# Two of a summed pair's four weight additions made by an accumulating DMA from DRAM, and eight raw weight slabs in flight instead of seven

## The chip, the core and the metric

The kernel runs on one core of a Trainium2 chip. The metric is device time in microseconds for one execution, the median of several runs. Engines are named as in the profile: PE (TensorE matmuls), PEld (its weight loads), DVE (VectorE), ACT (ScalarE), POOL (GpSimd) and SP (which only issues transfers here).

## The reference, cut to what matters

A trunk of two layers over 256 positions of width 2048, in float32. Each layer is a mixer followed by a feed-forward block; the change touches the feed-forward blocks alone.

```python
D_MODEL, SEQ, DEPTH = 2048, 256, 2
D_FF = 4 * D_MODEL

def rmsnorm(x, g):
    y = x * lax.rsqrt(jnp.mean(x * x, axis=-1, keepdims=True) + EPS)
    return y * g

for l in range(DEPTH):
    g = norm_g[l]
    u = rmsnorm(h, g[0])
    ...
    h = h + rmsnorm(y, g[1])
    u = rmsnorm(h, g[2])
    z = jnp.square(jax.nn.relu(u @ mlp_w1[l])) @ mlp_w2[l]
    h = h + rmsnorm(z, g[3])
```

## The kernel before

**Precision.** The weights come as float32. Every weight slab is split into a rounded part `whi`, which ScalarE makes by a cast, and the residual `wlo`, which VectorE makes by subtracting `whi` from the raw slab. A product then takes three matmuls: left high with `whi`, left high with `wlo`, left low with `whi`.

**Tiling.** A raw slab holds 128 partitions by two rows of 512 columns, 512 KB. Raw slabs live in a pool of `RAW_BUFS` buffers (line 25), which SP fills ahead of use. `whi` and `wlo` have `W_BUFS` = 6 buffers each (line 26). A buffer is free again when TensorE has made its last product with it, so ScalarE and VectorE can run at most six such tiles ahead of TensorE.

**The feed-forward block.** The hidden width of 8192 is cut into eight chunks of 1024 columns. The loop in `mlp` runs the up projection of chunk c, then the down projection of chunk c-1. Chunk 0 uses plain blocks; chunks 1 to 7 of each layer, 14 in all, use the class `Pairs` for the up projection. The down projection (class `Block`, lines 220 to 238) takes 16 slabs, each with one cast (L223), one residual (L224) and 12 matmuls (L236 to L238).

**Pairs.** The up projection of a chunk walks over eight pairs of k tiles in the order of the string `PAIRS = "CSCSSCSS"`. One pair is a 2 by 2 block of weight tiles (two k tiles, two halves of 512 columns, L and R) times a 2 by 2 block of activations (two k tiles, two halves of the positions). A C pair makes it conventionally, with 8 products (24 matmuls). An S pair, called a summed pair here, makes it in Strassen's manner with 7 products (21 matmuls), which need sums of weight tiles. For these, `Pairs.load` does the following. The raw slabs L and R are loaded (L327). L is split as it is (`plain`), and of R the second row (`r1`). Then four additions on VectorE (line 336) build the sums in place: R's second row takes R's first, R's first row takes L's first, L's first row takes the new second row of R, and L's second row takes the new first row of L. The new R is split (`two`) after the second addition, and the new L (`four`) after the last. So a summed pair fills four weight buffers, in the order plain, r1, two, four, and a C pair fills two. The casts are line 331 and the residuals line 332.

`Pairs.mm` makes the products (L357 to L359). A summed pair begins with the two products of `plain`, then one of `r1`, two of `two` and two of `four`. After the last pair of a chunk, VectorE and ScalarE combine the sums into the four blocks of the result (L372, L383, L387, L397, L398, L598).

**What sets the order.** The kernel is written as one program, and a scheduler lays it out on the engines. Each engine then runs its list in order: an instruction that waits holds up everything behind it on that engine. POOL issues nothing in the chunks before the change; its list there is empty between the stores of `mid` and `hsave` (L532).

Of the kernel before, what the change touches and what calls it, by code (L numbers as in the profile page):

```python
# [14 lines left out]
ALU = mybir.AluOpType  # L15
# [6 lines left out]
EPS = 1e-6  # L22
NT = 2
SLAB = 2
RAW_BUFS = 7
W_BUFS = 6
LEAD = 6
PAIRS = "CSCSSCSS"
# [11 lines left out]
def trunk(ctx, tc, x, x_t, norm_g, ng_cols, e_win, rbf, e_wout, o_win, lbraw, smalls, wa2, ba, o_wout, w1, w2,  # L40
          c_ident, c_flip, c_mask, out):
    nc = tc.nc
# [3 lines left out]
    x2p = ctx.enter_context(tc.tile_pool(name="x2p", bufs=8))  # L46
    rawp = ctx.enter_context(tc.tile_pool(name="rawp", bufs=RAW_BUFS))
    wp = ctx.enter_context(tc.tile_pool(name="wp", bufs=W_BUFS))
# [153 lines left out]
    def w_pair():  # L202
        return [wp.tile([P, SLAB, 512], F32R, name="w" + n) for n in ("hi", "lo")]

    class Block:
# [7 lines left out]
        def load(self, s):  # L213
            k0 = self.kts[s * SLAB]
            raw = rawp.tile([P, SLAB, 512], F32, name="raw")
            hi, lo = w_pair()
            n = slice(0, self.n)
            fine = s in self.fine
            for a, b in ((0, 1), (1, 2)) if fine else ((0, SLAB),):
                nc.sync.dma_start(out=raw[:, a:b, n], in_=self.wv[:, k0 + a:k0 + b, self.n0:self.n0 + self.n])  # L220
                if fine:
                    self.beside[a]()
                nc.scalar.copy(out=hi[:, a:b, n], in_=raw[:, a:b, n])  # L223
                nc.vector.tensor_tensor(out=lo[:, a:b, n], in0=raw[:, a:b, n], in1=hi[:, a:b, n], op=ALU.subtract)  # L224
            self.w[s] = (hi, lo)
# [84 lines left out]
    class Pairs:  # L310
# [13 lines left out]
        def load(self, s):  # L324
            raws = [rawp.tile([P, SLAB, 512], F32, name="raw") for _ in range(2)]
            for raw, n in zip(raws, (self.n0, self.n0 + 512)):
                nc.sync.dma_start(out=raw, in_=self.wv[:, 2 * s:2 * s + 2, n:n + 512])  # L327

            def conv(raw, i=slice(0, SLAB)):
                hi, lo = w_pair()  # L330
                nc.scalar.copy(out=hi[:, i, :], in_=raw[:, i, :])  # L331
                nc.vector.tensor_tensor(out=lo[:, i, :], in0=raw[:, i, :], in1=hi[:, i, :], op=ALU.subtract)  # L332
                return hi, lo

            def add(dst, a, b):
                nc.vector.tensor_tensor(out=dst, in0=a, in1=b, op=ALU.add)  # L336

            L, R = raws
            if PAIRS[s] == "C":
                self.w[s] = [conv(L), conv(R)]  # L340
                return
            plain = conv(L)
            r1 = conv(R, slice(1, 2))
            add(R[:, 1, :], R[:, 1, :], R[:, 0, :])
            add(R[:, 0, :], R[:, 0, :], L[:, 0, :])
            two = conv(R)
            add(L[:, 0, :], L[:, 0, :], R[:, 1, :])
            add(L[:, 1, :], L[:, 1, :], L[:, 0, :])
            self.w[s] = [plain, r1, two, conv(L)]
# [863 lines left out]
```

## Time and profile before

| | |
|---|---|
| median of 3 runs | 2261.35 us (2261.01 to 2261.88) |
| the profiled execution's own time | 2261.99 us |
| its span, first to last instruction | 2260.2 us |
| granted TensorE clock | 0.999 |
| ACT busy / DVE busy, share of the span | 52% / 77% |
| read from DRAM, whole span | 430.57 MB |

The span is shorter than the execution's time by 1.8 us, which lie around it. TensorE's matmuls overlap: a row's duration is longer than the distance between the starts of two neighbours, so the pace of TensorE is read from the distance of starts and not from the busy share. In a timeline, a row that ends in "x4" stands for four instructions in a row on that engine, and a bracket shows for how long the engine had been idle and what released it.

### The profile page before, as it was taken

The numbers are of one execution on the slowest core, as the hardware profiler recorded it, in microseconds if no ns is written. First come the engines' busy times: TensorE is split into PE (matmuls) and PEld (weight loads), VectorE is DVE, ScalarE is ACT, GpSimd is POOL, SyncE is SP. The second block draws the span as 40 slices with busy tenths as digits, with TensorE's granted clock in tenths as the row PEclk, the third lists the DMA queues.
The fourth block names the chain that finished last, engine by engine and source line by source line (L and its number), as shares of the span: only waits on it lengthen the run. The fifth ranks groups of instructions, "written<-read, shape, count | busy, mean of one in ns | idle before, by whom it ended". The sixth has DMA issues, their size and how long they took to land.

```text
span 2260.2 us, 28830 instructions
## 1 busy us (share of the span) xinstructions
PE 2238.3 (99%) x10556; PEld 1850.9 (82%) x10556; DVE 1750.7 (77%) x2328; ACT 1173.7 (52%) x1612; POOL 20.7 (1%) x40
## 2 busy tenths in 40 slices
PE   9999999999999999999999999999999999999998
PEld 7888887888888888888788888887888888888886
DVE  6656656988898898896867767657979789789786
ACT  7444445655454454454746454546555445445453
POOL 0000000000000000000100000000000000000000
PEclk9999999999999999999999999999999999999999
DMA  9565576565665665676655555576565565665673
GB/s 344 168 182 168 168 268 186 181 222 165 198 216 160 211 198 184 205 242 221 213 172 166 153 151 153 173 237 194 169 205 195 187 206 184 197 205 177 214 263 102
DMA packets 222559, 440.87 MB, mean 195 GB/s; under 512 B 13744, under 2 KB 14544, under 8 KB 222416
## 3 DMA queue, kind: packets, MB, share of 16 engines
q1 hardware_dynamic: 218880, 429.18, 59.1%
q0 software_dynamic: 2816, 8.99, 1.1%
q8 instruction: 83, 1.36, 0.3%
q10 hardware_dynamic: 720, 0.85, 0.1%
q14 instruction: 60, 0.49, 0.1%
HBM read 430.57 MB, written 8.40 MB: 194 GB/s over the span
## 4 chain that ended last, share of the span: by engine, by line
PE 75%; DVE 14%; issue 5%; ACT 4%; DMA 1%; ACTq 0%; DVEq 0%; SPq 0%
PE acc L237 18%; PE acc L238 17%; PE acc L236 17%; DVE raw L336 4%; DVE wlo L332 4%; PE acc L275 3%; PE aux L275 3%; ACT whi L331 3%; DVE wlo L224 2%; PE aux L272 2%; PE acc L272 2%; DVE ulo L383 2%; PE aux L359 2%; PE aux L357 2%; PE aux L358 2%
## 5 line engine op out<-in xcount | busy, mean ns | idle before, releaser
L224 DVE TENSOR_TENSOR wlo<-raw,whi 128x1024 fp32r<-128x1024 f32 (+1 forms) x561 | 676.2, 1219 | 303.9 <-ACT whi L223 301.9
L223 ACT CAST whi<-raw 128x1024 fp32r<-128x1024 f32 (+1 forms) x561 | 582.5, 1053 | 587.1 <-PE acc L238 464.7
L331 ACT CAST whi<-raw 128x1024 fp32r<-128x1024 f32 x364 | 343.5, 969 | 372.3 <-DVE raw L336 213.8
L237 PE MATMUL acc<-wlo,x 128*128 128x512 f32 x1280 | 502.7, 393 | 1.9 <-DVE wlo L224 0.6
L238 PE MATMUL acc<-whi,x 128*128 128x512 f32 x1280 | 498.8, 390 | 0.0
L236 PE MATMUL acc<-whi,x 128*128 128x512 f32 x1280 | 497.1, 392 | 0.0
L332 DVE TENSOR_TENSOR wlo<-raw,whi 128x1024 fp32r<-128x1024 f32 x364 | 397.9, 1119 | 106.2 <-ACT whi L331 99.4
L237 PEld LDWEIGHTS acc<-wlo,x 128*128 128x128 f32 x1280 | 240.3, 188 | 59.2 <-DVE wlo L224 10.8
L236 PEld LDWEIGHTS acc<-whi,x 128*128 128x128 f32 x1280 | 240.3, 188 | 50.6
L238 PEld LDWEIGHTS acc<-whi,x 128*128 128x128 f32 x1280 | 240.4, 188 | 49.1
L236 PE MATMUL acc<-whi,xt 128*128 128x512 f32 x640 | 254.1, 399 | 0.5 <-ACT xt L671 0.5
L237 PE MATMUL acc<-wlo,xt 128*128 128x512 f32 x640 | 251.6, 394 | 3.0 <-DVE wlo L224 3.0
L238 PE MATMUL acc<-whi,xt 128*128 128x512 f32 x640 | 250.8, 392 | 0.0
L336 DVE TENSOR_TENSOR raw<-raw 128x512 f32<-128x512 f32 x280 | 193.8, 692 | 9.3
L237 PEld LDWEIGHTS acc<-wlo,xt 128*128 128x128 f32 x640 | 120.8, 189 | 29.6 <-DVE wlo L224 6.2
L236 PEld LDWEIGHTS acc<-whi,xt 128*128 128x128 f32 x640 | 120.6, 189 | 25.7 <-ACT xt L671 1.4
L238 PEld LDWEIGHTS acc<-whi,xt 128*128 128x128 f32 x640 | 120.5, 188 | 25.3 <-issue 0.3
L357 PE MATMUL acc<-whi,xt 128*128 128x512 f32 x308 | 120.0, 390 | 0.0
L359 PE MATMUL acc<-whi,xt 128*128 128x512 f32 x308 | 119.8, 389 | 0.0
L358 PE MATMUL acc<-wlo,xt 128*128 128x512 f32 x308 | 119.8, 389 | 0.0
L358 PE MATMUL aux<-wlo,s 128*128 128x512 f32 x280 | 110.6, 395 | 1.9 <-DVE wlo L332 0.2
L357 PE MATMUL aux<-whi,s 128*128 128x512 f32 x280 | 109.2, 390 | 0.0
(230 smaller groups left out, 2551.2 us busy)
## 6 DMA issues: line engine op xcount, KB each, us to landing
raw<-w SPq DMA_DIRECT2D x512, 512.0 KB, 4.5
raw<-o_win SPq DMA_DIRECT2D x112, 512.0 KB, 3.8
raw<-e_win SPq DMA_DIRECT2D x95, 512.0 KB, 3.9
raw<-e_wout SPq DMA_DIRECT2D x32, 512.0 KB, 4.2
raw<-o_wout SPq DMA_DIRECT2D x32, 512.0 KB, 3.7
s<-norm_g SPq DMA_DIRECT2D x8, 512.0 KB, 4.6
mid<-s POOLq DMA_DIRECT2D x8, 512.0 KB, 3.5
s<-mid SPq DMA_DIRECT2D x8, 512.0 KB, 5.7
```

The source lines that it names most:

```text
L223: nc.scalar.copy(out=hi[:, a:b, n], in_=raw[:, a:b, n])
L224: nc.vector.tensor_tensor(out=lo[:, a:b, n], in0=raw[:, a:b, n], in1=hi[:, a:b, n], op=ALU.subtract)
L236: nc.tensor.matmul(ps, xh, hi[:, i, 0:self.n], start=first, stop=False)
L237: nc.tensor.matmul(ps, xh, lo[:, i, 0:self.n], start=False, stop=False)
L238: nc.tensor.matmul(ps, xl, hi[:, i, 0:self.n], start=False, stop=last)
L275: nc.tensor.matmul(self.ps[j], hi[:, i, cs], x, start=s == 0 and i == 0, stop=False)
L331: nc.scalar.copy(out=hi[:, i, :], in_=raw[:, i, :])
L332: nc.vector.tensor_tensor(out=lo[:, i, :], in0=raw[:, i, :], in1=hi[:, i, :], op=ALU.subtract)
L336: nc.vector.tensor_tensor(out=dst, in0=a, in1=b, op=ALU.add)
L357: nc.tensor.matmul(ps, xh, hi[:, i, :], start=first, stop=False)
L358: nc.tensor.matmul(ps, xh, lo[:, i, :], start=False, stop=False)
L359: nc.tensor.matmul(ps, xl, hi[:, i, :], start=False, stop=done and not (n == "bR" and i == 0))
```

## The change

Of the four additions of a summed pair, the first two are replaced by one transfer, issued by POOL, that reads a row of 1024 columns of the weight from DRAM again and adds it to the whole slab R in place. The row holds what L's first row and R's first row held when they were loaded, so the slab receives the same sums. The transfer writes R's second row, which `r1` reads, and so it starts after `r1`'s cast and residual. The other two additions stay on VectorE. Separately, the pool of raw slabs grows from seven buffers to eight.

```diff
-RAW_BUFS = 7
+RAW_BUFS = 8
...
             plain = conv(L)
             r1 = conv(R, slice(1, 2))
-            add(R[:, 1, :], R[:, 1, :], R[:, 0, :])
-            add(R[:, 0, :], R[:, 0, :], L[:, 0, :])
+            nc.gpsimd.dma_start(out=R.rearrange("p a b -> p (a b)"), in_=self.wv[:, 2 * s, self.n0:self.n0 + 1024],
+                                accum_op=ALU.add)
             two = conv(R)
             add(L[:, 0, :], L[:, 0, :], R[:, 1, :])
             add(L[:, 1, :], L[:, 1, :], L[:, 0, :])
             self.w[s] = [plain, r1, two, conv(L)]
```

The new transfer has line 344 in the changed kernel; the two additions that stay, the casts and the residuals keep lines 336, 331 and 332.

VectorE's list before the change, in the fifth of the first layer's paired chunks: the second summed pair and the beginning of the third. Slab raw_6904 is L and raw_6905 is R of the second pair, raw_6949 and raw_6950 are those of the third.

```order
L332 TENSOR_TENSOR wlo_6909<-raw_6904,whi_6908 128x1024
L332 TENSOR_TENSOR wlo_6913<-raw_6905,whi_6912 128x512
L336 TENSOR_TENSOR raw_6905<-raw_6905 128x512
L336 TENSOR_TENSOR raw_6905<-raw_6905,raw_6904 128x512
L336 TENSOR_TENSOR raw_6904<-raw_6904,raw_6905 128x512
L336 TENSOR_TENSOR raw_6904<-raw_6904 128x512
L332 TENSOR_TENSOR wlo_6919<-raw_6905,whi_6918 128x1024
L332 TENSOR_TENSOR wlo_6925<-raw_6904,whi_6924 128x1024
L332 TENSOR_TENSOR wlo_6954<-raw_6949,whi_6953 128x1024
L332 TENSOR_TENSOR wlo_6958<-raw_6950,whi_6957 128x512
```

The same place on VectorE in the changed kernel; here raw_6883 and raw_6884 are L and R of the second pair, raw_6927 and raw_6928 those of the third.

```order
L332 TENSOR_TENSOR wlo_6888<-raw_6883,whi_6887 128x1024
L332 TENSOR_TENSOR wlo_6892<-raw_6884,whi_6891 128x512
L336 TENSOR_TENSOR raw_6883<-raw_6883,raw_6884 128x512
L336 TENSOR_TENSOR raw_6883<-raw_6883 128x512
L332 TENSOR_TENSOR wlo_6897<-raw_6884,whi_6896 128x1024
L332 TENSOR_TENSOR wlo_6903<-raw_6883,whi_6902 128x1024
L332 TENSOR_TENSOR wlo_6932<-raw_6927,whi_6931 128x1024
L332 TENSOR_TENSOR wlo_6936<-raw_6928,whi_6935 128x512
L336 TENSOR_TENSOR raw_6927<-raw_6927,raw_6928 128x512
L336 TENSOR_TENSOR raw_6927<-raw_6927 128x512
```

Two of the four rows of line 336 are gone, and nothing else has taken their place: the first addition that is left reads R's new second row, and it stands directly behind the residual that the transfer waits for.

ScalarE's list in the changed kernel, from the same second summed pair to the end of the third; its order is the one that it had.

```order
L331 CAST whi_6887<-raw_6883 128x1024
L331 CAST whi_6891<-raw_6884 128x512
L331 CAST whi_6896<-raw_6884 128x1024
L331 CAST whi_6902<-raw_6883 128x1024
L331 CAST whi_6931<-raw_6927 128x1024
L331 CAST whi_6935<-raw_6928 128x512
L331 CAST whi_6940<-raw_6928 128x1024
L331 CAST whi_6946<-raw_6927 128x1024
```

The third row casts R after the transfer, and the two casts of the next pair (raw_6927, raw_6928) stand behind it and behind the cast of the summed L.

TensorE's list in the third summed pair before the change, from the first product with the summed R (whi_6963, wlo_6964) to the end; whi_6969 and wlo_6970 are the summed L.

```order
L357 MATMUL aux_6853<-whi_6963,s_3866 128x512
L358 MATMUL aux_6853<-wlo_6964,s_3866 128x512
L359 MATMUL aux_6853<-whi_6963,s_3866 128x512
L357 MATMUL aux_6857<-whi_6963,s_3866 128x512
L358 MATMUL aux_6857<-wlo_6964,s_3866 128x512
L359 MATMUL aux_6857<-whi_6963,s_3866 128x512
L357 MATMUL aux_6861<-whi_6969,s_3866 128x512
L358 MATMUL aux_6861<-wlo_6970,s_3866 128x512
L359 MATMUL aux_6861<-whi_6969,s_3866 128x512
L357 MATMUL aux_6805<-whi_6969,xt_3430 128x512
L358 MATMUL aux_6805<-wlo_6970,xt_3430 128x512
L359 MATMUL aux_6805<-whi_6969,xt_3430 128x512
```

The same place in the changed kernel, where whi_6940 and wlo_6941 are the summed R, and whi_6946 and wlo_6947 the summed L.

```order
L357 MATMUL aux_6832<-whi_6940,s_3866 128x512
L357 MATMUL aux_6836<-whi_6940,s_3866 128x512
L357 MATMUL aux_6840<-whi_6946,s_3866 128x512
L358 MATMUL aux_6832<-wlo_6941,s_3866 128x512
L359 MATMUL aux_6832<-whi_6940,s_3866 128x512
L358 MATMUL aux_6836<-wlo_6941,s_3866 128x512
L359 MATMUL aux_6836<-whi_6940,s_3866 128x512
L357 MATMUL aux_6785<-whi_6946,xt_3430 128x512
L358 MATMUL aux_6840<-wlo_6947,s_3866 128x512
L359 MATMUL aux_6840<-whi_6946,s_3866 128x512
L358 MATMUL aux_6785<-wlo_6947,xt_3430 128x512
L359 MATMUL aux_6785<-whi_6946,xt_3430 128x512
```

The twelve matmuls are the same; the scheduler has put a product with the summed L's cast in third place, ahead of the first product with a residual.

## The prediction

> **What bounds the kernel now.** I read the page's busy line first, then the table of waits, then the timelines of PE, DVE and ACT through one up chunk of the feed-forward part (the stage that the change touches).
>
> ```profile
> PE 2238.3 (99%) x10556; PEld 1850.9 (82%) x10556; DVE 1750.7 (77%) x2328; ACT 1173.7 (52%) x1612; POOL 20.7 (1%) x40
> ...
> L336 DVE TENSOR_TENSOR raw<-raw 128x512 f32<-128x512 f32 x280 | 193.8, 692 | 9.3
> ```
>
> TensorE is busy for 99% of the span. L336 holds the four weight additions of a summed pair: 280 of them, so 70 summed pairs, five in each of 14 up chunks. Removing half of them takes 140 x 0.692 = 97 us from VectorE, and nothing directly from TensorE. What TensorE loses to VectorE now is small:
>
> ```profile
> ACT whi L331 <- DVE raw L336: 213.8, 110, 3.5
> ...
> PEld acc L237 <- DVE wlo L224: 17.1, 36, 1.6
> ...
> PEld aux L358 <- DVE wlo L332: 7.8, 14, 0.7
> ...
> PE acc L237 <- DVE wlo L224: 3.7, 9, 1.2
> ```
>
> ScalarE waits 213.8 us for the additions, but TensorE's own waits for VectorE's weight work add up to 17.1 + 7.8 + 3.7 = 28.6 us. That is all that a lighter VectorE can give back. The timeline of one chunk shows why the slack is nevertheless thin. The first matmul of each pair, C S C S S C S S, and the first one of the down projection behind them:
>
> ```profile
> 781.35 0.39 PE L357 MATMUL acc<-whi,xt 128*128 128x512 f32 x1
> ...
> 786.78 0.39 PE L357 MATMUL acc<-whi,xt 128*128 128x512 f32 x1
> ...
> 791.54 0.39 PE L357 MATMUL acc<-whi,xt 128*128 128x512 f32 x1
> ...
> 801.75 0.39 PE L357 MATMUL acc<-whi,xt 128*128 128x512 f32 x1
> ...
> 806.50 0.39 PE L357 MATMUL acc<-whi,xt 128*128 128x512 f32 x1
> ...
> 816.71 0.39 PE L357 MATMUL acc<-whi,xt 128*128 128x512 f32 x1
> ...
> 821.91 0.40 PE L236 MATMUL acc<-whi,x 128*128 128x512 f32 x1
> ```
>
> A summed pair takes 791.54 - 786.78 = 4.76 us for its 21 matmuls, 0.2265 us each (the 0.39 us of a row overlaps its neighbours); a C pair takes 5.43 us. The last summed pair ends at 821.91, with 0.4 us of waiting in it. Now VectorE in the same chunk:
>
> ```profile
> 777.49 2.87 DVE L336 TENSOR_TENSOR raw<-raw 128x512 f32<-128x512 f32 x4
> ...
> 791.34 2.87 DVE L336 TENSOR_TENSOR raw<-raw 128x512 f32<-128x512 f32 x4
> ...
> 801.60 6.51 DVE L332 TENSOR_TENSOR wlo<-raw,whi 128x1024 fp32r<-128x1024 f32 x6
> 808.15 2.87 DVE L336 TENSOR_TENSOR raw<-raw 128x512 f32<-128x512 f32 x4
> 810.94 4.22 DVE L332 TENSOR_TENSOR wlo<-raw,whi 128x1024 fp32r<-128x1024 f32 x4
> 815.20 2.87 DVE L336 TENSOR_TENSOR raw<-raw 128x512 f32<-128x512 f32 x4
> ```
>
> VectorE runs a summed pair in 815.20 - 808.15 = 7.05 us: 2.79 us of additions and 4.26 us of residuals (this pair's sums, then the next pair's L and r1). With a C pair between, the residuals take 808.15 - 801.60 = 6.55 us. So inside the chunk VectorE, at 7.05 us, is slower than TensorE, at 4.76, and lives on its lead of six weight buffers. **The chunk is two chains that just meet: any microsecond added to VectorE's cycle reaches TensorE by the third summed pair.**
>
> **What the change does to that cycle.** It removes two additions (1.40 us of each 2.79) and puts a transfer in their place: POOL may start it only when r1's residual has been taken, and the cast of the new R, both remaining additions and all that is queued behind them wait for it to land. The instruction order shows no other work moved into the gap: on DVE the next rows are the two additions, the two residuals of the sums and only then the next pair's L and r1; on ACT the cast of R is followed by that of L and only then by the next pair's. Both engines stand for the whole transfer. Call T the time from POOL's issue to the landing. A cycle then takes 1.40 + 4.26 + T = 5.66 + T, against 7.05: **the exchange breaks even at T = 1.4 us.** No row of 512 KB is near that:
>
> ```profile
> L797 POOL DMA_DIRECT2D raw<-rbf x2: 768/776/784, 20.2 to 71.2; - x2
> ...
> DMA to landing us min/median/max: 4.2/5.6/7.0
> ```
> ```profile
> L532 POOL DMA_DIRECT2D mid<-s x8: 533/540/586, 384.5 to 1563.7; - x8
> ...
> DMA to landing us min/median/max: 2.9/4.1/6.4
> ```
> ```profile
> L327 SPq DMA_DIRECT2D raw<-w x224: 367/368/1543, 408.7 to 2142.5; - x112
> ...
> DMA to landing us min/median/max: 3.5/4.4/8.3
> ```
> ```profile
> q1 hardware_dynamic: 218880, 429.18, 59.1%
> ```
>
> No accumulating transfer is in this trace, so T is bounded. POOL's only 512 KB load from DRAM needs 4.2 us at best; its stores 4.1 in the median. The accumulation must also fetch the old R. The queue row prices another 512 KB: 0.591 x 16 x 2260.2 us for 429.18 MB is 49.8 us of one engine for each MB, so 0.524 MB over 16 engines takes 1.6 us. I take **T = 4.2 + 1.6 = 5.8 us**. Low end: the fastest POOL transfer of 512 KB in any direction, 2.9 us. High end: twice the load, 8.4 us, which is also about the slowest weight load (8.3). The Trainium skill ("DMA: Bandwidth & Descriptors", section on the anatomy of a SWDGE DMA) fits such a transfer with 2.0 us plus bytes over 436 GB/s, an estimate of 3.2 us here; the load row, 4.2 at best, is above it.
>
> Now the chunk, by VectorE's chain, from the time where the chain starts:
>
> - First summed pair: r1's residual ends at 777.49, where the additions begin now. Landing at 777.5 + T = 783.3. TensorE wants its sums about 2 us after 786.78. No stall.
> - Second: VectorE reaches r1's residual 1.40 + 6.55 us after that landing, at 791.25. Now it does so at 791.34, since r1's cast waits for TensorE to free a buffer (row below). Landing at 791.4 + T.
> - Third (S directly behind S): issue 5.66 us later. Landing at 797.1 + 2T.
> - Fourth (a C pair between): issue 7.95 us later. Landing at 805.1 + 3T.
> - Fifth: issue 5.66 us later. Landing at 810.8 + 4T.
>
> ```profile
> 788.39 1.58 ACT L331 CAST whi<-raw 128x1024 fp32r<-128x1024 f32 x2 [0.30 <-PE acc L359]
> ...
> 801.79 4.42 ACT L331 CAST whi<-raw 128x1024 fp32r<-128x1024 f32 x5 [0.40 <-DVE raw L336]
> ```
>
> From the last landing to the end of the pair: two additions 1.40, 0.2 to the cast of the last sum (the 801.79 row follows additions that end at 801.60), the cast 1.05, ten matmuls from there 2.27, together 5.0 us with one handover. The fifth pair ends at 815.8 + 4T against 821.91: **delay 4T - 6.1 us for each chunk**, 17.1 us at T = 5.8. The down projection cannot win it back, because there TensorE itself sets the pace (its waits above are 17.1 + 3.7 us in all). Above T = 5.8 the first transfer delays the second too, and the slope is 5.
>
> Sum: 14 x 17.1 = 239 us. Added to the profiled execution's own 2261.99 us, that is 2501 us; this execution lies 0.6 us above the median of the runs, so **2500 us**.
>
> **Small edits.** The eighth raw slab can remove the waits for loads:
>
> ```profile
> ACT whi L223 <- DMA raw<-w: 10.3, 14, 1.6
> ```
>
> These are 14 short waits of ScalarE at the start of each down projection. At most TensorE's 17.1 + 3.7 = 20.8 us at that place goes with them; at least nothing, since VectorE's evacuation falls in the same stretch. I take 0: the last summed pair still ends with VectorE's residual of its fourth weight, so the down projection starts as tightly as now. The transfers add 70 x 0.524 = 36.7 MB of reads:
>
> ```profile
> 781.35:821.77 40.42, 40.29 (x178) 33.05 (x177) 36.20 (x42) 22.59 (x26) 0.00 (x0) 1.00 0.53 166
> ```
>
> In this window (the chunk) the DMA engines are 53% busy, so the added 5 x 1.6 us fit and what they cost is in T. POOL is empty here (0.00, x0), so no other issue is delayed. TensorE's new order in the stalled pairs (three casts' products first) is counted in the ten matmuls.
>
> **The rivals.**
> - *A short landing*, T from 2.9 to 4.2: for it speaks the 2.9 us store, against it that both loads and accumulation do more. 14 x (4 x 2.9 - 6.1) = 77 us: 2339 to 2412 us. The Trainium skill's fit, named above, belongs here: T = 3.2 would give 2356 as an estimate; the load row does not bear it out. Chance 9%.
> - *A slow accumulation*, T above 8.4: the unit that adds may be slower than a copy, and no row shows it. At 8.4 the delay is 4 x 8.4 - 6.1 + 2.6 = 30.1 us a chunk, 421 us: above 2683. Chance 8%.
> - *The wait is hidden, and VectorE's 97 us count*: the transfer lands before anyone needs it, from T below 1.4 us on. Then the most that TensorE gets back is the 28.6 us of waits: 2233 to 2262 us. For it speaks that VectorE is the slower chain in this stage; against it stand all three landing rows and the order of both engines. Chance 5%, of which 3% is faster by over 0.2% (about what a measurement of this kernel can tell from no change) and 2% within it.
>
> **How the numbers follow.** The forecast, T from 4.2 to 8.4, has 78%: 2412 to 2683. The range gives up about 12% below (the hidden wait and most of the short landing) and 8% above: 2400 to 2670. Faster 3%, same 2%, slower 95%.
>
> **What would show it.** In the changed profile: POOL's issues at L344, 70 of them, with landings near 5.8 us; waits of ACT L331 and DVE L336 for that transfer, some 70 each, of about T (less in the first pair of a chunk); TensorE idle before L357 or L358 of the third, fourth and fifth summed pair, some 7, 4 and 7 us (by the ends above); down projections as long as now; VectorE's busy time 97 us less. Wrong would be a landing outside 4.2 to 8.4, or waits of TensorE of more than half a microsecond in the first two summed pairs, which would mean that the lead of six buffers is less than I read.

## The result and the profile after

The changed kernel takes **2633.72 us** (median of 4 runs, 2628.49 to 2642.79) against 2261.26 us for the kernel before on the same chip: a ratio of 1.165, 95% interval 1.1621 to 1.168. The profiled execution's own time is 2628.49 us, its span 2626.7 us, its granted TensorE clock 0.946.

The busy line of the page of after, and three rows of its 40 slices (tenths of busy time, and of full clock):

```profile
PE 2354.8 (90%) x10556; PEld 1911.1 (73%) x10556; DVE 1656.2 (63%) x2188; ACT 1170.9 (45%) x1612; POOL 80.2 (3%) x110
...
PE   9999999788697887969999999997978889797888
...
PEclk9999999899898999979999999999989899898989
DMA  9556766666565665657655545665656656565673
```

VectorE is 94.5 us lighter, as it should be by the removed additions, and TensorE is no longer always busy: its share falls to 6 to 8 tenths in most slices that hold paired chunks, while the rest of the program reads as before. Its granted clock falls in many of the same slices. Here are rows from the table of waits of after, its row for the additions, and the new issue line with its landings:

```profile
ACT whi L331 <- DMA raw<-w: 466.1, 68, 11.6
DVE raw L336 <- DMA raw<-w: 414.9, 70, 10.1
...
PEld aux L357 <- ACT whi L331: 285.7, 95, 8.2
PE aux L357 <- ACT whi L331: 236.2, 95, 7.7
```
```profile
L336 DVE TENSOR_TENSOR raw<-raw 128x512 f32<-128x512 f32 x140 | 96.8, 692 | 416.9 <-DMA raw<-w 414.9
```
```profile
L344 POOL DMA_DIRECT2D raw<-w x70: 837/850/883, 429.6 to 2513.0; - x70
...
DMA to landing us min/median/max: 5.3/7.0/9.7
```

ScalarE and VectorE now stand 6 to 7 us at each of the 70 transfers (414.9/70 and 466.1/68), and TensorE waits for ScalarE's casts, where it waited for almost nothing. The transfer lands in 7.0 us.

One chunk, the sixth paired one of the first layer, shows the chain. First POOL's issues; the bracket is the idle time ahead and its releaser:

```profile
990.24 0.85 POOL L344 DMA_DIRECT2D raw<-w  x1 [55.31 <-DVE wlo L332]
1005.40 0.86 POOL L344 DMA_DIRECT2D raw<-w  x1 [14.32 <-DVE wlo L332]
1019.09 0.85 POOL L344 DMA_DIRECT2D raw<-w  x1 [12.83 <-DVE wlo L332]
1033.75 0.86 POOL L344 DMA_DIRECT2D raw<-w  x1 [13.81 <-DVE wlo L332]
1045.60 0.85 POOL L344 DMA_DIRECT2D raw<-w  x1 [10.99 <-DVE wlo L332]
```

Then ScalarE's casts of the five summed R, which start when the transfer has landed:

```profile
995.66 1.05 ACT L331 CAST whi<-raw 128x1024 fp32r<-128x1024 f32 x1 [6.44 <-DMA raw<-w]
...
1013.24 1.04 ACT L331 CAST whi<-raw 128x1024 fp32r<-128x1024 f32 x1 [10.03 <-DMA raw<-w]
...
1025.62 1.05 ACT L331 CAST whi<-raw 128x1024 fp32r<-128x1024 f32 x1 [8.35 <-DMA raw<-w]
...
1039.74 1.04 ACT L331 CAST whi<-raw 128x1024 fp32r<-128x1024 f32 x1 [4.65 <-DMA raw<-w]
...
1052.98 1.04 ACT L331 CAST whi<-raw 128x1024 fp32r<-128x1024 f32 x1 [6.75 <-DMA raw<-w]
```

Cast minus issue gives the five landings: 5.42, 7.84, 6.53, 5.99 and 7.38 us, 33.16 in all. Issue minus the cast before gives the work between: 9.74, 5.85, 8.13 and 5.86, 29.58 in all. Last, TensorE's rows with idle time in this chunk (those of the second, third, fourth and fifth summed pair), its first matmul of the chunk, and the first of the down projection:

```profile
993.84 0.39 PE L357 MATMUL acc<-whi,xt 128*128 128x512 f32 x1
...
1014.34 0.50 PE L357 MATMUL aux<-whi,s 128*128 128x512 f32 x1 [2.66 <-ACT whi L331]
1015.84 0.50 PE L358 MATMUL aux<-wlo,s 128*128 128x512 f32 x1 [1.00 <-DVE wlo L332]
...
1026.72 1.09 PE L357 MATMUL aux<-whi,s 128*128 128x512 f32 x2 [4.44 <-ACT whi L331]
1028.24 0.79 PE L357 MATMUL aux<-whi,s 128*128 128x512 f32 x1 [0.43 <-ACT whi L331]
...
1040.84 0.74 PE L357 MATMUL aux<-whi,s 128*128 128x512 f32 x2 [1.61 <-ACT whi L331]
1042.36 0.50 PE L357 MATMUL aux<-whi,s 128*128 128x512 f32 x1 [0.79 <-ACT whi L331]
...
1054.08 1.22 PE L357 MATMUL aux<-whi,s 128*128 128x512 f32 x2 [7.11 <-ACT whi L331]
1055.54 0.80 PE L357 MATMUL aux<-whi,s 128*128 128x512 f32 x1 [0.23 <-ACT whi L331]
...
1058.87 0.39 PE L236 MATMUL acc<-whi,x 128*128 128x512 f32 x1
```

The chunk's up projection lasts 1058.87 - 993.84 = 65.03 us, against 40.56 in the chunk of before that the prediction shows: 24.5 us more, of which 18.3 are idle time in these rows. Of the other 6.2 us, 2.8 are clock: 14 starts in this chunk lie 0.40 to 0.45 us apart instead of 0.2265, as a few rows behind the wait in the second summed pair show:

```profile
1016.18 0.39 PE L359 MATMUL aux<-whi,s 128*128 128x512 f32 x1
1016.41 0.42 PE L357 MATMUL aux<-whi,s 128*128 128x512 f32 x1
1016.64 0.61 PE L358 MATMUL aux<-wlo,s 128*128 128x512 f32 x1
1017.05 0.63 PE L359 MATMUL aux<-whi,s 128*128 128x512 f32 x1
1017.48 0.63 PE L357 MATMUL aux<-whi,s 128*128 128x512 f32 x1
```

The starts are 0.23 us apart, then 0.43. The rest of the 6.2 us lies around the waits: idle time is counted from the end of a row, and a row is longer than the distance of starts.

The copy at L372 stands once in each of the 14 paired chunks, so its first and last start measure 13 periods (before, then after):

```profile
L372 ACT COPY s<-acc x14: 571/580/582, 464.0 to 2150.3; 128x512 f32<-128x512 f32 x14
```
```profile
L372 ACT COPY s<-acc x14: 587/587/587, 474.0 to 2500.8; 128x512 f32<-128x512 f32 x14
```

2026.8 against 1686.3 us: **26.2 us a chunk**, and 14 x 26.2 = 367 us is the whole difference of the spans (366.5). Little is lost or gained outside these periods.

### The profile page after: what moved, and what is told of

Read it like the earlier page. It is cut to its first block, busy times and chain, and to the rows that moved or that the text cites. A ratio compares the mean times of both kernels' runs of the same rounds, so it can differ in the third digit from the quotient of the medians.

```text
span 2626.7 us, 28956 instructions
## 1 busy us (share of the span) xinstructions
PE 2354.8 (90%) x10556; PEld 1911.1 (73%) x10556; DVE 1656.2 (63%) x2188; ACT 1170.9 (45%) x1612; POOL 80.2 (3%) x110
## 5 line engine op out<-in xcount | busy, mean ns | idle before, releaser
L223 ACT CAST whi<-raw 128x1024 fp32r<-128x1024 f32 (+1 forms) x561 | 582.8, 1052 | 603.5 <-PE acc L238 492.3
L331 ACT CAST whi<-raw 128x1024 fp32r<-128x1024 f32 x364 | 335.6, 965 | 619.4 <-DMA raw<-w 466.1
L336 DVE TENSOR_TENSOR raw<-raw 128x512 f32<-128x512 f32 x140 | 96.8, 692 | 416.9 <-DMA raw<-w 414.9
L357 PE MATMUL aux<-whi,s 128*128 128x512 f32 x280 | 141.4, 534 | 236.2 <-ACT whi L331 236.2
L357 PEld LDWEIGHTS aux<-whi,s 128*128 128x128 f32 x280 | 60.3, 232 | 292.0 <-ACT whi L331 285.7
L236 PE MATMUL acc<-whi,xt 128*128 128x512 f32 x640 | 253.3, 398 | 1.8 <-ACT whi L223 0.9
L237 PE MATMUL acc<-wlo,xt 128*128 128x512 f32 x640 | 251.2, 393 | 2.7 <-DVE wlo L224 1.4
L238 PE MATMUL acc<-whi,xt 128*128 128x512 f32 x640 | 250.5, 392 | 0.0
L358 PE MATMUL aux<-wlo,s 128*128 128x512 f32 x280 | 139.8, 499 | 12.7 <-DVE wlo L332 12.7
L359 PE MATMUL aux<-whi,s 128*128 128x512 f32 x280 | 137.5, 491 | 0.0
L357 PE MATMUL acc<-whi,xt 128*128 128x512 f32 x308 | 123.2, 400 | 0.0
```

Of the source, the lines that this page charges most:

```text
L236: nc.tensor.matmul(ps, xh, hi[:, i, 0:self.n], start=first, stop=False)
L237: nc.tensor.matmul(ps, xh, lo[:, i, 0:self.n], start=False, stop=False)
L238: nc.tensor.matmul(ps, xl, hi[:, i, 0:self.n], start=False, stop=last)
L357: nc.tensor.matmul(ps, xh, hi[:, i, :], start=first, stop=False)
L358: nc.tensor.matmul(ps, xh, lo[:, i, :], start=False, stop=False)
L359: nc.tensor.matmul(ps, xl, hi[:, i, :], start=False, stop=done and not (n == "bR" and i == 0))
```

## The experiments

**The eighth slab alone.** The kernel before, with only the pool made larger.

```diff
-RAW_BUFS = 7
+RAW_BUFS = 8
```

> The kernel before with eight raw slabs and all four additions on VectorE. Theory (the wait for the transfer is the whole loss): 2255 to 2263 us, no transfer on POOL in the chunks, granted clock 0.999. Rival (the eighth slab, through other addresses or earlier loads, carries part of the loss): above 2290 us.

Measured: 2261.68 us, ratio 1.0 (0.9991 to 1.001). The eighth slab alone changes nothing in the time, although ScalarE's waits for loads at L223, 10.3 us before, are down to 0.3.

**The transfer with seven slabs.** The changed kernel with `RAW_BUFS` back at 7.

> The change with seven raw slabs. Theory (the wait): 2615 to 2650 us, as the change itself. Rival (the eighth slab matters once slabs are held for the transfer): more than 20 us away from the change's 2634 us.

Measured: 2630.18 us in one run, landing 7.1 us in the median, clock 0.948. The same as the change: the loss is the transfer's, and it makes no difference to it whether there are seven slabs or eight.

**A copy in place of the accumulation.** The same transfer without the addition.

```diff
-            nc.gpsimd.dma_start(out=R.rearrange("p a b -> p (a b)"), in_=self.wv[:, 2 * s, self.n0:self.n0 + 1024],
-                                accum_op=ALU.add)
+            nc.gpsimd.dma_start(out=R.rearrange("p a b -> p (a b)"), in_=self.wv[:, 2 * s, self.n0:self.n0 + 1024])
```

> The change with the same transfer without accumulation: R is overwritten by the row of DRAM, so the sums of the summed pairs are not formed from the old R. Every wait stays. Theory (the time follows the landing time T, about 4.5 chunk slopes x 14 = 63 us for each us of T): if a copy lands in 4.2 to 5.0 us instead of 7.0, 2460 to 2510 us. Rival (the accumulation itself costs nothing, T stays near 7): 2600 to 2640 us.

Measured: 2496.97 us, one run. The landings of this kernel:

```profile
DMA to landing us min/median/max: 3.6/4.8/7.5
```

So the accumulation costs 7.0 - 4.8 = 2.2 us of landing, and these 2.2 us cost 2633.7 - 2497.0 = 137 us: 62 us for each microsecond of T. The prediction's slopes of 4 and 5 in each of 14 chunks are 56 and 70. The time follows T as the chain says it should, and two thirds of T, and of the loss, would be there with a plain copy too.

The pages' rows of the software queue, which holds POOL's transfers, price the addition in another way: 9.2% of the span of 16 engines in the change, 5.4% here, 1.1% before. For the 36.7 MB added that is 94 us of one engine for each MB when it accumulates and 48 when it copies, so 3.1 and 1.6 us over 16 engines for one transfer. 1.5 of the 2.2 us are thus longer packets; the other 0.7 us stay open.

**A transfer that nobody waits for.** The first two additions are left out, and the transfers go into a slab of their own that is never read.

```diff
+    spares = [const.tile([P, 1024], F32, name="spare")]
...
-            nc.gpsimd.dma_start(out=R.rearrange("p a b -> p (a b)"), in_=self.wv[:, 2 * s, self.n0:self.n0 + 1024],
-                                accum_op=ALU.add)
+            spare = spares[0]
+            nc.gpsimd.dma_start(out=spare, in_=self.wv[:, 2 * s, self.n0:self.n0 + 1024], accum_op=ALU.add)
```

> The first two additions are left out, and the accumulating transfer goes, as often and as large, into one spare slab that nobody reads; seven raw slabs. The sums of the summed pairs lack these two additions. Theory (the loss is waiting alone; VectorE is 97 us lighter): 2233 to 2262 us. Rival (the transfers slow the other loads or the engines' ports): above 2350 us.

Measured: 2350.81 us, ratio 1.0395 (1.0379 to 1.041). The theory is missed; the rival's number is just reached, but not in the way that it meant. With nothing to wait for, the 70 transfers did not stay in their chunks. They ran one behind the other from the program's start, and the table of waits shows POOL standing for each before the next:

```profile
POOL spare L349 <- DMA spare<-w: 448.2, 68, 9.4
```

They crowd the start (DMA engines 86% busy from 1 to 230 us, against 67% before) and POOL's own loads there stand behind them. So it says nothing of transfers beside a chunk's work. It does show one thing, since the last transfer was issued at 522.2 us, before the first of these copies: the same copy of each chunk (L376 here).

```profile
L376 ACT COPY s<-acc x14: 580/581/582, 567.5 to 2239.9; 128x512 f32<-128x512 f32 x14
```

1672.4 us for 13 periods, 1.07 us less for each than before. **Two additions less on VectorE in each summed pair are worth 15 us here**, if nothing replaces them.

**The transfer ahead of its use.** R's second row is loaded twice. One copy serves `r1`; the other slab, which nothing reads before, is accumulated at once and becomes the summed R. In the program only the slab's load stands ahead of the transfer, and no cast or residual of its own pair. It needs three slabs for a summed pair instead of two, of eight in all.

```diff
-            raws = [rawp.tile([P, SLAB, 512], F32, name="raw") for _ in range(2)]
+            raws = [rawp.tile([P, SLAB, 512], F32, name="raw") for _ in range(2 if PAIRS[s] == "C" else 3)]
...
+            S = raws[2]
+            nc.gpsimd.dma_start(out=S.rearrange("p a b -> p (a b)"), in_=self.wv[:, 2 * s, self.n0:self.n0 + 1024],
+                                accum_op=ALU.add)
             plain = conv(L)
             r1 = conv(R, slice(1, 2))
-            nc.gpsimd.dma_start(out=R.rearrange("p a b -> p (a b)"), in_=self.wv[:, 2 * s, self.n0:self.n0 + 1024],
-                                accum_op=ALU.add)
+            R = S
```

> The change with the accumulating transfer taken off both engines' chains: R is loaded into a slab of its own and accumulated there as soon as it has been loaded, and r1 is taken from a third slab that holds R's second row alone. Nothing on VectorE or ScalarE has to end before the transfer starts. Theory (only the wait on the engines' chains costs time): the loss of 372 us goes, and VectorE is still 97 us lighter: 2240 to 2262 us. Rival (the transfers themselves are the bound, with 3.5 slabs of traffic for each summed pair and eight slabs in flight): 2270 to 2400 us, with waits for loads or for the transfer.

Measured: 2285.94 us (2273.72 to 2299.86), ratio 1.0101 (1.0047 to 1.0156), though the transfer is no quicker (7.2 us). So the rival's range holds and the theory's does not: most of the loss goes, but not all. ScalarE's waits for DMAs at its casts of the pairs:

```profile
ACT whi L332 <- DMA raw<-w: 83.4, 23, 7.0
```

**This is the test of the main theory.** The same 70 transfers, of the same size and slowness, cost 25 us instead of 372 when VectorE and ScalarE need not stand for them. ScalarE still waits in 23 places: these transfers come late. The same up projection as in the prediction's window, at its times in this kernel, with the share of the DMA engines and GB/s at its end:

```profile
792.54:835.94 43.40, 40.72 (x179) 33.14 (x178) 30.22 (x33) 22.95 (x26) 2.56 (x3) 1.00 0.80 235
```

The DMA engines are 80% busy, against 53% before, and the up projection's weight loads land in 5.3 us in the median, against 4.4. What makes the transfers late is not shown. Two readings point at the slabs more than at the traffic. Of POOL's 70 issues the table of waits puts 30 down to a load that landed and 35 to VectorE (17 and 4 residuals, 14 additions), as if slabs in use had run out. And the kernel with two such transfers a chunk, below, has its DMA engines 78% busy in the same up projection and loses nothing.

**Filling TensorE's idle time.** Products with a weight of zeros are put where TensorE waits, to keep its clock up. They add zero to a sum.

```diff
+            for _ in range({3: 8, 4: 16, 6: 4, 7: 28}.get(s, 0)):
+                nc.tensor.matmul(z["q5"], zero, d.hi.rearrange("p i n -> p (i n)"), start=False, stop=False)
```

> The change with TensorE kept busy in its waits: before the first product with the summed R, 8, 16, 4 and 28 matmuls with a weight of zeros (second to fifth summed pair) add nothing to an open sum. The granted clock should stay near 1. Theory A (TensorE's lower clock after a wait lengthens the chain only behind the last landing of a chunk, about 1 us each): 2605 to 2632 us. Theory B (all of the lost clock counts, 5.4% of the span): 2480 to 2550 us.

Measured: 2646.78 us, ratio 1.1709 (1.1678 to 1.174), with the clock at 0.976 instead of 0.946; neither theory's range holds. The clock rose and the time did not fall, which speaks against theory B. In the trace of after, 372 starts lie 0.40 to 0.45 us apart, 74 us more than at 0.2265. Where the next landing is still to come, such lost time only shortens the wait for it; that is argued from the chain. How much the clock costs stays open: the scheduler laid out the real products in another order in this kernel, and some waits still had a low clock behind them.

**Half the transfer.** Only R's second half is accumulated by the transfer (256 KB); VectorE keeps the other addition.

```diff
-            nc.gpsimd.dma_start(out=R.rearrange("p a b -> p (a b)"), in_=self.wv[:, 2 * s, self.n0:self.n0 + 1024],
-                                accum_op=ALU.add)
+            nc.gpsimd.dma_start(out=R[:, 1, :], in_=self.wv[:, 2 * s, self.n0 + 512:self.n0 + 1024], accum_op=ALU.add)
+            add(R[:, 0, :], R[:, 0, :], L[:, 0, :])
```

> The change with a transfer of half the size: only R's second row is accumulated by DMA, its first row's addition is back on VectorE, where it needs no transfer and fits into the wait. Theory (time follows T at about 60 us for each us, as between the change, T 7.0, and the plain copy, T 4.8): if T is the bytes, about 5 us and 2500 to 2530 us; if T is nearly all fixed, 6.5 us and 2590 to 2610 us.

Measured: 2521.11 us in one run. The landings:

```profile
DMA to landing us min/median/max: 3.9/4.8/7.4
```

Half the bytes land in 4.8 us instead of 7.0, so 2.6 us do not depend on the size and the other 4.4 do (by a line through the two points). The time is 24 us above the copy of the whole slab with the same 4.8 us. The addition that came back may be the reason: VectorE stops for a DMA 133 times at L336 here, 68 times with the copy. It was not tried apart.

**`r1` before `plain`.** The transfer is issued one cast and one residual earlier; both then have `plain` to do while it runs.

```diff
-            plain = conv(L)
             r1 = conv(R, slice(1, 2))
             nc.gpsimd.dma_start(out=R.rearrange("p a b -> p (a b)"), in_=self.wv[:, 2 * s, self.n0:self.n0 + 1024],
                                 accum_op=ALU.add)
+            plain = conv(L)
```

> The change with r1 taken first: the transfer is issued ahead of L's cast and residual, which then run while it is under way. Same work, same transfers. Theory (the engines stand for T minus what they can do meanwhile): 1.1 us less of standing in four to five pairs of each of 14 chunks, 2550 to 2575 us. Rival (the transfers' load on the DMA engines or on memory sets the pace): 2615 us or more.

Measured: 2599.41 us in one run, landing 7.5 us. The gain, 34 us, has the expected sign and is more than the 14 us by which runs of the change differ, but it is about half the expected size. The transfer itself was 0.5 us slower here, which by the 62 us for each microsecond costs 31 us; that would account for the missing half, but why it lands later was not tried. Neither expectation's range holds.

**Ahead of its use, where it can be hidden.** Two kernels with the third slab as above, in some of the summed pairs only; the others keep four additions on VectorE. In the first it is the fifth summed pair of a chunk, in the second the third and the fifth, which stand directly behind another summed pair. The diff is the first kernel's against the one with the transfer ahead in all five; the second has `AHEAD = (4, 7)`.

```diff
+AHEAD = (7,)
...
-            raws = [rawp.tile([P, SLAB, 512], F32, name="raw") for _ in range(2 if PAIRS[s] == "C" else 3)]
+            raws = [rawp.tile([P, SLAB, 512], F32, name="raw") for _ in range(3 if s in AHEAD else 2)]
...
-            R = S
+            if s in AHEAD:
+                R = raws[2]
+            else:
+                add(R[:, 1, :], R[:, 1, :], R[:, 0, :])
+                add(R[:, 0, :], R[:, 0, :], L[:, 0, :])
```

> Only the fifth summed pair of a chunk gets its two sums by the transfer into a third slab that nothing has read yet, so that the transfer starts as soon as the slab is loaded; the other four pairs keep all four additions on VectorE. 14 transfers instead of 70. Theory A (the loss was the wait on the engines' chains, and what is left of it with five transfers a chunk is raw slabs that come late): one transfer a chunk is hidden, and VectorE's chain in the last pair is 1.40 us shorter, where TensorE waits 0.4 us in the kernel before. Between 14 x 0.4 = 6 us faster and no change: 2255 to 2262, waits for the transfer under 5 us in all. Rival B (each such transfer costs whatever the slabs do, by its traffic): a fifth of the 25 us that five of them cost, 5 us, so 2266 or more. Rival C: it gives all of the 1.07 us a chunk that the kernel with two additions left out gained where no transfer ran: 15 us, 2246.

> As with one transfer ahead of use, but in the third and the fifth summed pair of a chunk, those that stand directly behind another summed pair, where VectorE's chain is slower than TensorE: 28 transfers. Theory A (hidden while slabs suffice): VectorE is 2.8 us lighter where it is behind; between 15 us faster, the 1.07 us a chunk that the kernel with two additions left out gained where no transfer ran, and no change: 2246 to 2262. Rival B (a price for each transfer): two fifths of 25 us, 10 us, so 2271 or more, and slower than with one transfer a chunk. If the waits of ScalarE and VectorE for the transfer are above 20 us in all, slabs are already short with two.

Measured: one transfer a chunk 2279.40 us, ratio 1.008 (1.0066 to 1.0094), so slower; two transfers a chunk **2247.89 us, ratio 0.9941 (0.9929 to 0.9954)**, 14 us faster than the kernel before and the fastest here. So rival B's number holds for one transfer, but a price for each transfer would make two dearer than one, and is refuted. With two, the copy of each chunk:

```profile
L380 ACT COPY s<-acc x14: 573/578/581, 463.7 to 2136.2; 128x512 f32<-128x512 f32 x14
```

1672.5 us for 13 periods: all of the 1.07 us a chunk that the two left-out additions gave, from two pairs of five. The wait of TensorE's weight loads in the down projection, 17.1 us before, is nearly gone:

```profile
PEld acc L238 <- DVE wlo L225: 3.4, 6, 1.0
```

So the two pairs where VectorE's chain is slower than TensorE's give as much as all five did. In most chunks the up projection falls from 40.56 us to 40.12 and the down projection from 46.1 to 45.4.

One transfer alone loses 18 us, more than any of the three expectations gave a reason for. Issue and use in the fifth summed pair of one chunk, first with one transfer a chunk, then with two:

```profile
722.82 0.84 POOL L345 DMA_DIRECT2D raw<-w  x1 [87.13 <-DMA raw<-w]
```
```profile
731.06 1.05 ACT L333 CAST whi<-raw 128x1024 fp32r<-128x1024 f32 x1 [1.82 <-DMA raw<-w]
```
```profile
715.39 0.85 POOL L345 DMA_DIRECT2D raw<-w  x1 [18.84 <-DMA raw<-w]
```
```profile
723.67 1.05 ACT L333 CAST whi<-raw 128x1024 fp32r<-128x1024 f32 x1 [1.01 <-DMA raw<-w]
```

The landing is alike, 8.2 and 8.3 us. Both are late, but one waits 1.82 us after what was done before and the other 1.01; ScalarE is ready 6.4 us after the issue in the first, 7.3 in the second. In all, it waits 28.4 us (14 times) with one and 13.4 (12 times) with two. The larger difference stands behind the landing, in the order of VectorE's list and ScalarE's cast of the summed L, again with one and then with two:

```profile
732.14 1.22 DVE L334 TENSOR_TENSOR wlo<-raw,whi 128x1024 fp32r<-128x1024 f32 x1 [1.38 <-ACT whi L333]
733.28 1.41 DVE L338 TENSOR_TENSOR raw<-raw 128x512 f32<-128x512 f32 x2
...
734.81 1.05 ACT L333 CAST whi<-raw 128x1024 fp32r<-128x1024 f32 x1 [2.70 <-DVE raw L338]
```
```profile
723.66 1.41 DVE L338 TENSOR_TENSOR raw<-raw 128x512 f32<-128x512 f32 x2
...
725.18 1.05 ACT L333 CAST whi<-raw 128x1024 fp32r<-128x1024 f32 x1 [0.46 <-DVE raw L338]
```

With one, the scheduler put the residual of the summed R ahead of the two additions, so the summed L's cast starts 3.75 us after the summed R's; with two, the additions come first, and it is 1.51. Counted from the chunk's copy (L380 here, L372 before), that cast starts at 8.56 us with one and at 7.54 in the kernel before: 1.02 us later, and the time between two chunks' copies is 1.0 us longer in most chunks. The loss with one is thus mostly this order, as far as these rows show; the same kernel with the additions first was not tried.

## Why the prediction was right, and where its sizes were off

The forecast was 2500 us and the range 2400 to 2670; measured 2633.72. Sign and mechanism hold, and the size is 134 us short.

- **The wait is on two chains.** ScalarE stands 68 times and VectorE 70 times for the transfer, TensorE stands for ScalarE. With the wait taken away (the transfer ahead of its use), 372 us become 25.
- **T, the landing, was the term most mis-sized.** It was taken as the fastest POOL load (4.2) plus 1.6 us for the accumulation. The copy measures 4.8 in these chunks, the accumulation 2.2 more: 7.0, within the bounds of 2.9 to 8.4. The 1.6 us agree with the 1.5 that the packets of an accumulation take longer; the 0.6 us of the load and the rest of the 2.2 were missed. At the prediction's own slope of 5 the 1.2 us are 6.0 us a chunk, 84 us in all. Single landings left the range that was to hold: 5 of the 70, all in the last paired chunk of a layer, took 8.5 to 9.7 us.
- **The first cycle was longer than counted.** From the first landing to the second issue the prediction had 7.95 us, the chunk shows 9.74. There the summed R's residual and an evacuation (L611) stand between the two additions that are left, so the summed L comes later. Its order was assumed to be that of the pairs further on. The other three cycles are 0.2 us longer than worked out (5.85, 8.13, 5.86 against 5.66, 7.95, 5.66). Together 2.4 us a chunk.
- **No term for the clock.** From the last landing to the chunk's end the prediction had 5.0 us; the chunk shows 1058.87 - 1052.98 = 5.89. The matmuls there start 0.43 us apart for a while. 0.9 us in this chunk, the least of the 14; on the mean it is 6.7 us, 1.7 more than predicted.
- **The sum with these three.** In the chunk shown the landings are 6.63 us on the mean, 0.83 above 5.8, so the sum is 17.1 + 4.2 + 2.4 + 0.9 = 24.6 us, and its up projection is 24.5 longer. Over all 14 chunks the mean landing is 6.87, and a down projection is 0.6 us shorter than before, for which the prediction had nothing: 17.1 + 5.4 + 2.4 + 1.7 - 0.6 = 26.0 us a chunk, measured 26.2.
- **Where TensorE waits.** The prediction named 7, 4 and 7 us in the third, fourth and fifth summed pair; the chunk shows 4.9, 2.4 and 7.3, and 3.7 in the second. It had named waits above half a microsecond in the first two pairs as a sign that the lead of six buffers is less than read. It was not that: the second landing is late by a longer T and the longer first cycle.
- **The small edits.** The eighth slab at nothing: shown. The down projections are no longer than before; the weight loads' waits for VectorE there even fall, from 17.1 to 3.9 us. VectorE's additions are 97.0 us less (193.8 to 96.8), all of VectorE 94.5.
- **The rivals.** The hidden wait (T under 1.4 us) did not occur: no landing was under 5.3 us. It does occur, in another form, when the transfer is issued ahead, and gives 14 us, half of the 28.6 that were its ceiling. That ceiling was a loose one: it adds waits of weight loads, which overlap matmuls, to waits of matmuls. With two transfers ahead the same rows fall to 4.7 us, by 23.9, for 14 us gained. The slow accumulation begins at T = 8.4, the short landing ends at 4.2; the median is between them.

## What to carry to other kernels

Before additions go from an engine to a transfer, see what the engine that gives them up has in its list until the landing. Here it had nothing, and the transfer's whole latency stood in the place of the additions, 7.0 us for 1.40. Compare the latency with the shortest cycle of the chain that waits, find out what the transfer must wait for, and remove that first (a second copy of 256 KB did). Then use it only where the engine relieved is the one behind: here two pairs of five gave 14 us, and all five lost 25. Read the order of the lists again after such an edit: with the fifth pair alone, a residual that moved ahead of two additions went with a loss of 18 us.

## What the runs showed of the hardware that was not expected

- An accumulating transfer of 512 KB from DRAM lands in 7.0 us (median of 70), the same transfer as a copy in 4.8, an accumulating one of 256 KB in 4.8. POOL is busy for 0.85 us with the issue of an accumulation, with 512 KB as with 256; the copy took 0.53.
- The packets of an accumulating transfer take about twice the time of a copy's, 94 against 48 us of one DMA engine for each MB.
- TensorE's clock falls after short waits. In the second summed pair 2.66 us and 1.00 us of idle time, with one recorded matmul between, were followed, three starts later, by eight starts 0.43 us apart instead of 0.23, that is, half the pace. The Trainium skill ("TensorE: Matmul & The Clock Gate", section on how the oscillation bites in real kernels) warns of idle gaps above some 3.4 us. The trace shows that less is enough: each of the two gaps is shorter. The Trainium skill ("TensorE: Matmul & The Clock Gate", section on what is actually happening) gives two clocks only, half and full. The trace agrees: its clock records hold 1 and 0.5 alone, and the two paces are 0.43 and 0.23. In the whole run half the clock lasted 3.4, 6.8 or 10.2 us at a time, 45 times, and once more at the end of the span, 282 us in all; the granted clock of the whole run fell from 0.999 to 0.946.
